# One decoder layer on TensorE: reading the moving operand and writing the result of the block products from the last column to the first

## The chip, the cores and the metric

The kernel runs on one core of one Trainium2 chip, as one program. The time is the device time of one execution in microseconds (us). The time before is the median of two runs. The trace and its page come from one profiled execution; its time is given as its span, from the first to the last instruction.

## The reference, cut to what matters

A hybrid decoder layer over 16 meta tokens and 512 tokens of width 2048, in float32: an input projection, stick-breaking attention in 8 heads beside a gated short convolution of 1024 channels, an output projection and a SwiGLU feed-forward part of width 5632.

```python
n = _rmsnorm(h, g_mix[l])
p = n @ w_in[l]
q, k, v, gb, gc, u = jnp.split(p, ...)
...
o_attn = _stick_breaking_attention(q, k, v).reshape(b, L, ATTN_WIDTH)
o_conv = gb * _causal_dwconv(gc * u, conv_w[l])
o = jnp.concatenate([_rmsnorm(o_attn, g_attn_out[l]), _rmsnorm(o_conv, g_conv_out[l])], axis=-1)
h = h + o @ w_out[l]
n2 = _rmsnorm(h, g_ffn[l])
h = h + (jax.nn.silu(n2 @ w_gate[l]) * (n2 @ w_up[l])) @ w_down[l]
```

Nearly all of the arithmetic is in the products with `w_in`, `w_out`, `w_gate`, `w_up` and `w_down`.

## The kernel before, in words

Everything is kept transposed: 128 channels of one tile lie on the 128 partitions, the tokens along the row. A weight tile of 128 x 128 is the stationary operand of TensorE, activations are the moving operand, and products add up in PSUM over the tiles of the contracted dimension.

Each float32 operand is split into a high part, rounded to the float32r type, and a low part, what the rounding left (`split_quad` for weights, lines 196 to 211: ScalarE casts at line 203, VectorE subtracts at line 206; `split` for activations, lines 352 to 353). A product of two such operands is three matmuls: high by high, high by low, low by high.

The big products also save work in the manner of Strassen's and Winograd's method. Weights and activations are cut into two by two blocks, and seven products of sums of blocks take the place of eight. `pair_product` (line 900) issues the seven in a fixed order into three PSUM banks named `x`, `y` and `z`: `x` gets blocks 0, 2, 4 and 6, `z` gets 1 and 3, `y` gets 5. Between them ScalarE and VectorE read out what has been added up so far. Each of the seven is one call of `block_product` (line 871), the function that the change edits. It takes the next prepared weight block (`next_w`, a running list of pieces, each split some places ahead of its use into the tiles `sw_split`), and for each tile `k` of the contracted dimension issues the three matmuls at lines 887, 890 and 891: `hi` by `ah`, `hi` by `al`, `lo` by `ah`. [...] `act(0, k)` and `act(1, k)` give the high and low part of the moving operand's tile `k`, each with 256 or 258 columns.

The stages that go through `block_product`:

- the convolution pairs (`conv_pair`, `gate_pair`, about 385 to 588 us of the trace): moving operands from the tiles `n` (rows of 528 columns that begin 40 places into their tile) and `mixed`, 258 columns for `conv_pair` and 256 for `gate_pair`;
- gate and up of the feed-forward part (`ffn_pair` from the loop over 44 blocks, about 764 to 1603 us): moving operands `f`, seven sets of eight tiles of 256 columns, which `slots` puts 4 places into their tile;
- down (about 1603 to 2022 us): moving operands `first` and `ring`, four or six tiles of 256 columns, read back from DRAM.

With the quarter of the weights that `two_down` prepares, two output halves lie in one bank of 512 columns and `block_product` loops over both (`m` is 2). The head projections (`product_steps`, lines 340 and 342) and the output projection (`wide_product`, lines 865 to 867) have loops of their own with the same three matmuls, mostly 512 columns wide; they are not edited. In `product_steps` the tile `pq` is made from columns 16 to 528 of the rows `n`. In `gate_pair` the bank `y` is made from columns 16 to 272 of those of them that hold the second half of the channels.

Of the kernel before, what the change touches and what calls it, by code (L numbers as in the profile page):

```python
# [33 lines left out]
def hybrid_layer(ctx: ExitStack, tc: tile.TileContext, xT, w_in, w_out, w_gu, w_down, vecs, out):  # L34
# [269 lines left out]
    def next_w():  # L304
        ahead = max(min(n_first, used[0] + 6), used[0] + 1 + S_AHEAD)
        if used[0] < n_first:
            ahead = min(ahead, n_first + 1)
        while len(split_w) < min(len(pieces), ahead):
            if n_first < len(split_w) <= n_first + S_AHEAD:
                with tc.issue_after(read_q0[3].ins):  # L310
                    prepare()
            else:
                prepare()
        used[0] += 1
        return split_w[used[0] - 1]
# [555 lines left out]
    def block_product(ps, act, start):  # L871

        hi, lo = next_w()
        i = pieces[used[0] - 1][1]
        m = max(1, ps.shape[-1] // T2)
        cols = ps.shape[-1] // m  # L880
        n = pairs[i][0] // m
        for j in range(m):
            p, skip = ps[:, j * cols : (j + 1) * cols], m > 1 or not start
            for k in range(n):
                kk = slice((j * n + k) * P, (j * n + k + 1) * P)
                ah, al = act(0, k), act(1, k)
                opening = pe.matmul(p, hi[:, kk], ah, start=start and j == k == 0, stop=False, skip_group_check=skip)  # L887
                if j == k == 0:
                    tc.keep_in_program_order(opening)
                pe.matmul(p, hi[:, kk], al, start=False, stop=False, skip_group_check=skip)  # L890
                pe.matmul(p, lo[:, kk], ah, start=False, stop=k == n - 1, skip_group_check=skip)  # L891
# [8 lines left out]
    def pair_product(acts, cols, out2, side, fifth=None, hook=None):  # L900
# [16 lines left out]
        if first:  # L917
            block_product(y, acts[5], True)
            go_between()
        block_product(x, acts[0], True)  # L920
        read_out(p1, x)
        go_between()
        if hook:
            hook(1)
        block_product(z, acts[1], True)
        go_between()
        read_out(p5, z)
# [134 lines left out]
    for i, j in enumerate(OUT_TILES):  # L1062
# [36 lines left out]
        ps = ps_out[i]  # L1099
        half, k = divmod(j, 8)  # L1100
# [313 lines left out]
```

## Time and profile before

| what | value |
|---|---|
| median of 2 runs | 2027.59 us (2027.51 to 2027.67) |
| span of the profiled execution | 2025.8 us |
| TensorE: time with a matmul in flight, instructions | 2019.7 us, 16158 |
| weight loads (PEld) | 1961.8 us, 16158 |
| VectorE | 1723.3 us |
| ScalarE | 1077.9 us |
| GpSimd | 337.3 us |
| read from HBM, written to it | 275.78 MB, 77.92 MB |

How to read it. The profile has a row for each instruction: line, engine, operation, the tile written and the tiles read, the shape. Matmuls are pipelined, so the row of one overlaps the next ones' rows: one of 256 columns is in flight for 275 ns, yet the next starts long before that. What a matmul costs the stream is the distance between starts, which is read from the timeline (start times in us) or from a window's length over its count of instructions. Weight loads have rows of their own under the name PEld and overlap the matmuls. In the timeline, rows of one form that follow each other can be merged, with their count after the x.

### The profile page before, as it was taken

Reading aid. Unit: us, or ns where it says so; the run is one execution under the profiler, and the core shown is the slowest. Engines: PE = TensorE matmul, PEld = TensorE weight load, DVE = VectorE, ACT = ScalarE, POOL = GpSimd, SP = SyncE. Lnnn points to the kernel's source line nnn. Section 1 sums busy time; section 2 is a strip of 40 time slices with the busy share of each in tenths; the row PEclk is TensorE's granted clock in tenths of the full one; section 3 lists DMA queues with packets and bytes.
Section 4 is the critical chain, followed back from the end, with each engine's and each line's share of the span. In section 5 each row is a group of like instructions: output and inputs, shape, how many; then the busy total and the mean of one; then the engine's idle time right before and its main releaser. Section 6 shows DMA issues by size and latency. Waiting matters only on the chain.

```text
span 2025.8 us, 39704 instructions
## 1 busy us (share of the span) xinstructions
PE 2019.7 (100%) x16158; PEld 1961.8 (97%) x16158; DVE 1723.3 (85%) x2199; ACT 1077.9 (53%) x1559; POOL 337.3 (17%) x507
## 2 busy tenths in 40 slices
PE   9999999999999999999999999999999999999999
PEld 8999999999998889999999999999999999999999
DVE  7877777698877778999988988988988978888888
ACT  7876676444454445555555555555555544444443
POOL 0111111200014440111110110110110243131211
PEclk9999999999999999999999999999999999999999
DMA  6333343833255555556554554554554999797864
GB/s 222 116 135 115 125 136 136 282 105 110 99 198 179 165 161 194 171 153 186 173 160 148 167 164 149 164 166 151 162 166 151 290 339 352 170 318 193 222 149 91
DMA packets 156664, 356.31 MB, mean 176 GB/s; under 512 B 13696, under 2 KB 68224, under 8 KB 155712
## 3 DMA queue, kind: packets, MB, share of 16 engines
q1 hardware_dynamic: 72640, 216.73, 32.2%
q0 software_dynamic: 83696, 136.99, 25.0%
q8 instruction: 127, 2.08, 0.4%
q14 instruction: 57, 0.47, 0.1%
q10 hardware_dynamic: 144, 0.04, 0.0%
HBM read 275.78 MB, written 77.92 MB: 175 GB/s over the span
## 4 chain that ended last, share of the span: by engine, by line
PE 99%; DMA 0%; DVE 0%; SPq 0%; ACT 0%; issue 0%
PE x L887 14%; PE x L891 14%; PE x L890 14%; PE z L887 7%; PE z L890 7%; PE z L891 7%; PE y L891 3%; PE y L887 3%; PE y L890 3%; PE pk L342 3%; PE pv L342 3%; PE pq L342 3%; PE pv L340 2%; PE pk L340 2%; PE pq L340 1%; PE pb L342 1%
## 5 line engine op out<-in xcount | busy, mean ns | idle before, releaser
L203 ACT CAST sw_split<-sw_in 128x1024 fp32r<-128x1024 f32 (+3 forms) x671 | 662.4, 989 | 708.7 <-PE x L890 174.2
L206 DVE TENSOR_TENSOR sw_split<-sw_in,sw_split 128x1024 fp32r<-128x1024 f32 (+3 forms) x671 | 775.5, 1156 | 140.4 <-ACT sw_split L203 133.0
L887 PE MATMUL x<-f,sw_split 128*128 128x256 f32 x1408 | 387.5, 275 | 0.1
L891 PE MATMUL x<-f,sw_split 128*128 128x256 f32 x1408 | 387.2, 275 | 0.0
L890 PE MATMUL x<-f,sw_split 128*128 128x256 f32 x1408 | 387.2, 275 | 0.0
L887 PEld LDWEIGHTS x<-f,sw_split 128*128 128x128 f32 x1408 | 264.3, 188 | 0.7 <-DVE u L937 0.5
L890 PEld LDWEIGHTS x<-f,sw_split 128*128 128x128 f32 x1408 | 264.3, 188 | 0.0
L891 PEld LDWEIGHTS x<-f,sw_split 128*128 128x128 f32 x1408 | 264.3, 188 | 0.0
L1206 POOL DMA_DIRECT2D fd<-s x147 | 103.7, 921 | 708.0 <-DVE s L353 632.1
L887 PE MATMUL z<-f,sw_split 128*128 128x256 f32 x704 | 193.6, 275 | 0.0
L890 PE MATMUL z<-f,sw_split 128*128 128x256 f32 x704 | 193.6, 275 | 0.0
L891 PE MATMUL z<-f,sw_split 128*128 128x256 f32 x704 | 193.6, 275 | 0.0
L216 DVE TENSOR_TENSOR sw_in<-sw_in 128x1024 f32<-128x1024 f32 (+1 forms) x164 | 187.7, 1145 | 5.4 <-DMA sw_in<-w_in 0.8
L887 PE MATMUL x<-ring,sw_split 128*128 128x256 f32 x608 | 167.2, 275 | 0.0
L890 PE MATMUL x<-ring,sw_split 128*128 128x256 f32 x608 | 167.2, 275 | 0.0
L891 PE MATMUL x<-ring,sw_split 128*128 128x256 f32 x608 | 167.2, 275 | 0.0
L890 PEld LDWEIGHTS z<-f,sw_split 128*128 128x128 f32 x704 | 132.2, 188 | 0.0
L891 PEld LDWEIGHTS z<-f,sw_split 128*128 128x128 f32 x704 | 132.2, 188 | 0.0
L887 PEld LDWEIGHTS z<-f,sw_split 128*128 128x128 f32 x704 | 132.2, 188 | 0.0
L887 PEld LDWEIGHTS x<-ring,sw_split 128*128 128x128 f32 x608 | 114.1, 188 | 0.0
L891 PEld LDWEIGHTS x<-ring,sw_split 128*128 128x128 f32 x608 | 114.1, 188 | 0.0
L890 PEld LDWEIGHTS x<-ring,sw_split 128*128 128x128 f32 x608 | 114.1, 188 | 0.0
(701 smaller groups left out, 5276.9 us busy)
## 6 DMA issues: line engine op xcount, KB each, us to landing
sw_in<-w_gu SPq DMA_DIRECT2D x176, 512.0 KB, 3.8
sw_in<-w_in SPq DMA_DIRECT2D x90, 512.0 KB, 3.3
fd<-s POOLq DMA_DIRECT2D x147, 256.0 KB, 5.1
sw_in<-w_down SPq DMA_DIRECT2D x96, 384.0 KB, 4.2
ring<-fd POOLq DMA_DIRECT2D x42, 768.0 KB, 17.6
sw_in<-w_out SPq DMA_DIRECT2D x32, 512.0 KB, 3.3
out_T<-d POOLq DMA_DIRECT2D x54, 256.0 KB, 4.6
mix_dram<-st_x POOLq DMA_DIRECT2D x16, 516.0 KB, 4.1
```

Of the source, the lines that this page charges most:

```text
L203: cast[0] = sc.copy(hi, src)
L206: latest[0] = ve.tensor_tensor(lo, src, hi.bitcast(F32), ALU.subtract)
L216: return ve.tensor_tensor(sums[name], a, b, ALU.add)
L340: pe.matmul(ps, wh, ah[:, a:b], start=k + i == 0, stop=False)
L342: pe.matmul(ps, w, x[:, a:b], start=False, stop=k + i == last and x is (al if used[0] <= n_first else ah))
L887: opening = pe.matmul(p, hi[:, kk], ah, start=start and j == k == 0, stop=False, skip_group_check=skip)
L890: pe.matmul(p, hi[:, kk], al, start=False, stop=False, skip_group_check=skip)
L891: pe.matmul(p, lo[:, kk], ah, start=False, stop=k == n - 1, skip_group_check=skip)
L1206: gp.dma_start(fd[c][s][:, :, k], t[:, :, i])
```

## The change

In `block_product` the view of the PSUM bank that is written, and the views of both parts of the moving operand, get a step of -1 along the columns. Column 255 of the operand is then read first and its sum is written first, to place 255 of the output; column 0 comes last. Each column's sum goes to the address where it went before. The weights' views, the number of instructions, and all that surrounds the function are the same.

```diff
         n = pairs[i][0] // m
         for j in range(m):
-            p, skip = ps[:, j * cols : (j + 1) * cols], m > 1 or not start
+            p, skip = ps[:, j * cols : (j + 1) * cols][:, ::-1], m > 1 or not start
             for k in range(n):
                 kk = slice((j * n + k) * P, (j * n + k + 1) * P)
-                ah, al = act(0, k), act(1, k)
+                ah, al = (act(i, k)[:, ::-1] for i in range(2))
                 opening = pe.matmul(p, hi[:, kk], ah, start=start and j == k == 0, stop=False, skip_group_check=skip)
```

## The prediction

> **What bounds the kernel now.** I read the page first, parts 1, 2 and 4, to see which engine sets the end.
>
> ```profile
> span 2025.8 us, 39704 instructions
> ...
> PE 2019.7 (100%) x16158; PEld 1961.8 (97%) x16158; DVE 1723.3 (85%) x2199; ACT 1077.9 (53%) x1559; POOL 337.3 (17%) x507
> ...
> PEclk9999999999999999999999999999999999999999
> ...
> PE 99%; DMA 0%; DVE 0%; SPq 0%; ACT 0%; issue 0%
> ```
>
> TensorE is busy in the whole span, its clock is granted at nine tenths or more in every slice (1.00 in the stretches below), and the chain that ended last lies on it for 99%. So the time is a number of matmuls times the distance from one start to the next. That distance, not the mean of one matmul, is the price: neighbours overlap. To get it I asked the view by windows for three stretches in which block products run, first for all instructions, then for those of line 890 alone, one of the three matmul lines of the edited function.
>
> ```profile
> core 0: us, PE busy (x) PEld busy (x) DVE busy (x) ACT busy (x) POOL busy (x), PEclk, DMA share, GB/s
> 385.20:588.00 202.80, 202.65 (x1686) 202.09 (x1685) 175.44 (x201) 98.19 (x129) 5.67 (x10) 1.00 0.41 139
> 764.00:1603.00 839.00, 838.90 (x7397) 838.28 (x7396) 757.57 (x856) 442.68 (x581) 115.11 (x163) 1.00 0.55 168
> 1603.00:2021.90 418.90, 418.90 (x3699) 418.90 (x3697) 364.64 (x467) 197.12 (x285) 89.59 (x106) 1.00 0.85 237
> ```
>
> ```profile
> 385.20:588.00 202.80, 158.28 (x560) 105.91 (x560) 1.00 0.41 139
> 764.00:1603.00 839.00, 677.52 (x2464) 462.56 (x2464) 1.00 0.55 168
> 1603.00:2021.90 418.90, 338.82 (x1233) 231.27 (x1232) 1.00 0.85 237
> ```
>
> Span over count: the convolution pairs (first stretch) take 202.80 us / 1686 = 120.3 ns per matmul, gate and up (second) 839.00 / 7397 = 113.4 ns, down (third) 418.90 / 3699 = 113.2 ns. By the counts of line 890, and three matmul lines, the function issues 3 x 560 = 1,680 matmuls in the first and 3 x (2,464 + 1,232) = 11,088 in the other two: 12,768 of the 16,158, 1,460 of the 2,026 us. A nanosecond on each of them is 12.8 us.
>
> Why do matmuls of one size, 256 columns, come 113 ns apart in one stage and 120 in another? The timeline shows it. First activations of the gate stage (`f`), then tiles `n` in the convolution pairs, twice, then the same `n` tiles with 512 columns in the head loop.
>
> ```profile
> 1002.07 0.28 PE L890 MATMUL z<-f,sw_split 128*128 128x256 f32 x1
> ...
> 1004.45 0.28 PE L890 MATMUL z<-f,sw_split 128*128 128x256 f32 x1
> ```
>
> ```profile
> 460.80 0.29 PE L887 MATMUL x<-n,sw_split 128*128 128x256 f32 x1
> 460.92 0.29 PE L890 MATMUL x<-n,sw_split 128*128 128x256 f32 x1
> 461.05 0.29 PE L891 MATMUL x<-n,sw_split 128*128 128x256 f32 x1
> 461.18 0.28 PE L887 MATMUL y<-n,sw_split 128*128 128x256 f32 x1
> ...
> 461.53 0.28 PE L887 MATMUL y<-n,sw_split 128*128 128x256 f32 x1
> ...
> 463.69 0.28 PE L887 MATMUL y<-n,sw_split 128*128 128x256 f32 x1
> ```
>
> ```profile
> 55.08 0.39 PE L340 MATMUL pq<-n,sw_split 128*128 128x512 f32 x1
> 55.31 0.61 PE L342 MATMUL pq<-n,sw_split 128*128 128x512 f32 x2
> ...
> 57.80 0.39 PE L340 MATMUL pq<-n,sw_split 128*128 128x512 f32 x1
> ```
>
> The 21 steps between the two `z<-f` rows take 2.38 us, 113.3 ns each. The 18 between the two later `y<-n` rows take 2.16 us, 120.0 ns each. The three steps from 460.80 to 461.18 take 0.38 us, 126.7 ns each. The twelve 512-column steps from 55.08 to 57.80 take 2.72 us, 226.7 ns each. The rows of `y` and of `pq` start at the same column of the same kind of tile and differ in length alone, so 256 more columns cost 226.7 - 120.0 = 106.7 ns, 0.417 ns a column. What is left is a fixed part of each matmul with its weight load: 120.0 - 106.7 = 13.3 ns for these reads, 20.0 ns for the ones at 460.80, and 6.7 ns for `f`. The streaming rate is the same; the fixed part goes by which operand is read. My reading, argued and not shown: each matmul hides the next one's weight load (PEld is busy 97%), both read SBUF, and where their reads meet the stream loses some cycles; how often they meet depends on where and in which order the moving operand is read.
>
> **The change, part by part.** Only access patterns change. No instruction, DMA, wait or buffer is added or moved, and no queue is passed by anything. Each output column gets the same sums at the same address, so the readers of PSUM do what they did.
>
> Moving operand, last column first. The columns streamed stay the same in number. If the read keeps its rate, the 106.7 ns stay; what changes is the meeting with the weight load, which keeps its own order. For that fixed part the trace gives the ends. Below: this row, where TensorE takes four 128-column products with their own weight loads.
>
> ```profile
> 53.79 0.60 PE L608 MATMUL va<-ident,v 128*128 128x128 f32 x4
> 54.23 0.27 PE L609 MATMUL vb<-ident,v 128*16 128x128 f32 x1
> ```
>
> They take 54.23 - 53.79 = 0.44 us, 110 ns each, so a weight load does not itself hold products to 113. Above: the 126.7 ns of `x<-n`. Between them lie the 120.0 ns of `y<-n` and the convolution pairs' mean of 120.3 over 1,686. The 113.3 of `f` is the lowest steady value of any 256-column row here, and it is one that was obtained in rising order. I take 120.0, the row of the same shape that is nearest to the mean of all operands not at that low value: 11,088 x (120.0 - 113.4) = +73 us. The convolution pairs are already at such a mean, so I cost them at nothing, with +/-10 us (1,680 x about 6 ns) as the bounds. The cover of these products is unharmed: everything beside them gets more time, and DVE, busiest beside them, had 839.00 - 757.57 = 81 us free in the gate stage.
>
> Result in PSUM, last column first. No row of before writes in falling order, so the cost is bounded only from afar. Below, a write is no slower, zero. Above, it halves the rate: another 106.7 ns for each 256 columns. I take zero, since the 13.3 ns above come out alike for 256 and 512 columns, so the write is not what limits them now, and a falling run touches the same neighbours; the upper end is a rival below.
>
> [...]
>
> Sum: 2025.8 + 73 = 2,099 us of span; the median of the runs, 2027.59, lies 1.8 us above the profiled span, so **2,101 us**. The reads cost more and nothing becomes late, since TensorE is the only engine on the path.
>
> **The rivals.**
>
> No effect: the fixed part depends on where the operand lies, not on its order, so 113.3 stays 113.3. For it: 256 columns cover the same bytes either way, and the `f`, ring and down rows all show that one value although they lie in many places. Against it: `x<-n` at 460.80 and `y<-n` at 461.53, same shape and kind of tile, differ by 6.7 ns, so something finer than shape counts. Time: 2,028 us, 2,018 to 2,038 with the convolution pairs' +/-10.
>
> Halved rate: the read or the write of a falling run goes at one column in two of the present steps. For it: nothing in this trace has been run in falling order, and 0.417 ns a column leaves no slack to hide a slower access. Against it: 256 columns of one row are still neighbours. Price: 12,768 x 106.7 ns = 1,362 us, so 3,390 us. It decides as soon as a column costs visibly more than 0.417 ns; an added 0.1 ns would already make 12,768 x 25.6 ns = 327 us.
>
> Faster: weight load and stream now run through SBUF in an order in which they meet less, so the fixed part falls. For it: 113.3 is not the floor that the 110 ns of `va` show. Against it: in all the `f` and ring rows the low value is the same, which looks like a minimum. Price: at 110 ns the FFN stages give back 11,088 x 3.4 = 38 us and the convolution pairs 1,680 x 10.3 = 17 us: 1,973 us. It decides from 2%, 41 us, on: with the pairs' 17 us the FFN rows must lose 24 us, 2.2 ns each, and without them 3.7 ns, which is 109.7. DVE would then come nearer to being the bound: 757.57 of what would be 814 us, 93%.
>
> [...]
>
> **How the numbers follow.** A few per cent is what has to be told apart, so I count within 2% as no change. More meetings, the forecast: 0.36, its own range 2,040 (the fixed part up by 1.1 ns) to 2,178 (all at 126.7 ns, +151 us). Of this 0.04 lies within 2%. No effect: 0.34, all within 2%. Halved rate: 0.20, all slower. Faster: 0.10, of which 0.01 stays within 2%. So slower 0.32 + 0.20 = 0.52, same 0.04 + 0.34 + 0.01 = 0.39, faster 0.09. The range leaves out the halved rate alone, 0.20: from 1,965, a little under the faster rival, to 2,180.
>
> **What would show it.** Right: the count of instructions stays at 16,158 matmuls, the `z<-f` rows of 256 columns come about 120 ns apart, 764 to 1603 us becomes some 49 us longer and the down stage 24 us, and the 512-column `pq` rows, not edited, stay at 226.7 ns. Wrong: the `f` rows still at 113.3 (no effect); rows over 200 ns apart with a mean well over 275 ns (halved rate); rows near 110 (faster). If the 256- and 258-column rows rise by an amount in proportion to columns, my split into a rate and a fixed part fails; if the matmuls keep 113 ns but idle time appears ahead of them, the whole reading by TensorE alone is wrong.

## The result, and the profile after

The changed kernel takes 2101.46 us (median of 2 runs, 2101.32 to 2101.60) against 2027.59 us: a ratio of 1.0364, interval 1.0334 to 1.0395. It is slower by 73.9 us; the forecast was 2,101 us.

The page after, parts 1 and 4: the same count of instructions on every engine that computes, the same engine on the chain. The span of the profiled execution is 2099.9 us.

```profile
PE 2094.7 (100%) x16158; PEld 2036.5 (97%) x16158; DVE 1732.2 (82%) x2199; ACT 1076.8 (51%) x1559; POOL 338.2 (16%) x507
...
PE 99%; DVE 1%; issue 0%; ACT 0%; DVEq 0%
```

The three stretches by windows, all instructions, with the columns of the windows of before; the granted clock is 1.00 in each, as it was. The last two have the same work as in the windows shown of before; their ends moved to 1652.2 and 2096.1 us.

```profile
385.20:588.00 202.80, 202.65 (x1684) 202.17 (x1683) 174.97 (x200) 97.62 (x128) 5.68 (x10) 1.00 0.41 138
764.00:1652.20 888.20, 888.15 (x7399) 887.71 (x7399) 766.11 (x856) 441.55 (x581) 115.30 (x163) 1.00 0.52 159
1652.20:2096.10 443.90, 443.90 (x3700) 443.75 (x3698) 365.00 (x467) 197.27 (x285) 89.83 (x106) 1.00 0.81 223
```

Span over count: 202.80 / 1684 = 120.4 ns in the convolution pairs (120.3 before), 888.20 / 7399 = 120.0 ns in gate and up (113.4), 443.90 / 3700 = 120.0 ns in down (113.2). Gate and up are 49.2 us longer, down is 25.0 us longer; with nothing from the pairs that makes 74.2, and the span grew by 2099.9 - 2025.8 = 74.1 us. No other group of rows moved the end by as much as 1 us. The timeline, first in the gate stage, then in `gate_pair`, then the 512-column products that were not edited:

```profile
1001.96 0.28 PE L887 MATMUL y<-f,sw_split 128*128 128x256 f32 x1
...
1004.12 0.28 PE L887 MATMUL y<-f,sw_split 128*128 128x256 f32 x1
...
461.03 0.28 PE L887 MATMUL x<-n,sw_split 128*128 128x256 f32 x1
...
461.39 0.28 PE L887 MATMUL y<-n,sw_split 128*128 128x256 f32 x1
...
55.11 0.39 PE L340 MATMUL pq<-n,sw_split 128*128 128x512 f32 x1
...
57.83 0.39 PE L340 MATMUL pq<-n,sw_split 128*128 128x512 f32 x1
```

The 18 steps in `y<-f` take 2.16 us, 120.0 ns each, where 113.3 stood. The last three reads of the block `x<-n` went from 126.7 (at 460.80 before) to 0.36 us / 3 = 120.0 ns. `pq` keeps its 2.72 us for twelve, 226.7 ns. So falling order did not add a constant to what was there: it took the fast rows and some of the slowest ones to the same 120.0 ns.

### The profile page after: what moved, and what is told of

It is laid out like the page before. It is cut to its first block, busy times and chain, and to the rows that moved or that the text cites. A ratio compares the mean times of both kernels' runs of the same rounds, so it can differ in the third digit from the quotient of the medians.

```text
span 2099.9 us, 39735 instructions
## 1 busy us (share of the span) xinstructions
PE 2094.7 (100%) x16158; PEld 2036.5 (97%) x16158; DVE 1732.2 (82%) x2199; ACT 1076.8 (51%) x1559; POOL 338.2 (16%) x507
## 4 chain that ended last, share of the span: by engine, by line
PE 99%; DVE 1%; issue 0%; ACT 0%; DVEq 0%
PE x L887 14%; PE x L891 14%; PE x L890 14%; PE z L887 7%; PE z L890 7%; PE z L891 7%; PE y L891 3%; PE y L887 3%; PE y L890 3%; PE pk L342 3%; PE pv L342 3%; PE pq L342 3%; PE pv L340 2%; PE pk L340 1%; PE pq L340 1%; PE pb L342 1%
## 5 line engine op out<-in xcount | busy, mean ns | idle before, releaser
L887 PE MATMUL x<-f,sw_split 128*128 128x256 f32 x1408 | 400.0, 284 | 0.1
L891 PE MATMUL x<-f,sw_split 128*128 128x256 f32 x1408 | 399.9, 284 | 0.0
L890 PE MATMUL x<-f,sw_split 128*128 128x256 f32 x1408 | 399.9, 284 | 0.0
L887 PE MATMUL z<-f,sw_split 128*128 128x256 f32 x704 | 199.9, 284 | 0.0
L890 PE MATMUL z<-f,sw_split 128*128 128x256 f32 x704 | 199.9, 284 | 0.0
L891 PE MATMUL z<-f,sw_split 128*128 128x256 f32 x704 | 199.9, 284 | 0.0
L887 PE MATMUL x<-ring,sw_split 128*128 128x256 f32 x608 | 172.7, 284 | 0.0
L890 PE MATMUL x<-ring,sw_split 128*128 128x256 f32 x608 | 172.7, 284 | 0.0
L891 PE MATMUL x<-ring,sw_split 128*128 128x256 f32 x608 | 172.7, 284 | 0.0
```

## The experiments

Three theories at the start. Mine: the read of the moving operand meets the weight load's reads in SBUF, and order and place of the read set how often. The rivals: the write in falling order costs it; or falling order costs the read by itself, with no part of the weights in it.

**Read alone, write alone.** Each undoes one half of the change.

```diff
# e1_read                                      (of the changed kernel)
-            p, skip = ps[:, j * cols : (j + 1) * cols][:, ::-1], m > 1 or not start
+            p, skip = ps[:, j * cols : (j + 1) * cols], m > 1 or not start
# e2_write
-                ah, al = (act(i, k)[:, ::-1] for i in range(2))
+                ah, al = act(0, k), act(1, k)
```

> Only the moving operand is read from the last column to the first; the result is written in rising order (so each block's columns come out mirrored). Theory, the read's order against the weight load's: as the changed kernel, 2101 us, within 5 us, and gate-stage rows 120.0 ns apart. Rival, the falling write in PSUM costs the 6.7 ns: as before, 2028 us and rows 113.3 ns apart.

> Only the result is written from the last column to the first; the moving operand is read in rising order (columns mirrored). Theory, the read's order: as before, 2028 us, within 5 us, rows 113.3 ns apart. Rival, the falling write: 2101 us and 120.0 ns.

Read alone: 2101.48 us, ratio 1.0365 (1.035 to 1.038). Write alone: 2027.60 us against 2027.56, ratio 1.000 (0.999 to 1.0009). The gate stage of the one and of the other, in the timeline:

```profile
1001.97 0.28 PE L887 MATMUL y<-f,sw_split 128*128 128x256 f32 x1
...
1004.13 0.28 PE L887 MATMUL y<-f,sw_split 128*128 128x256 f32 x1
```

```profile
1001.88 0.28 PE L887 MATMUL z<-f,sw_split 128*128 128x256 f32 x1
...
1004.26 0.28 PE L887 MATMUL z<-f,sw_split 128*128 128x256 f32 x1
```

18 steps in 2.16 us, 120.0 ns; 21 steps in 2.38 us, 113.3 ns. The whole cost is in the read, none in the write: a written step of -1 did not slow these matmuls.

**Other places, rising and falling.** The operands of the feed-forward stages start at another offset in their tiles, a different one for each slot, so one run shows many. Offsets are in elements from the tile's start; 4 is that of before. The tiles are laid out in multiples of 64 elements (256 bytes), so an offset means the same place against the weights in each of them.

```diff
+    PLACE = {"f0": 0, "f1": 2, "f2": 6, "f3": 8, "f4": 20, "f5": 36, "f6": 52, "first1": 12, ...}
-        t = t[:, 4 : 4 + c].rearrange("p (s a k t) -> p s a k t", s=m, a=2, k=n)
+        at = PLACE.get(name, 4)
+        t = t[:, at : at + c].rearrange("p (s a k t) -> p s a k t", s=m, a=2, k=n)
```

The pad ahead of `f4` had to shrink too, so that slot lies as if at offset 28. The same edit was made to the changed kernel, and both were run again with eighteen further offsets, each version once.

> Rising order as before, but each set of activations of the feed-forward stages starts at another place in its tile (0 to 64 elements instead of 4), so each of the seven block products shows its own distance between matmuls. Theory, the read meets the weight load by place and order: the low 113.3 ns is kept by some places alone, others give 118 to 127 ns; the whole lies between 2040 and 2120 us. Rival, order alone counts: every place shows 113.3 ns, 2028 us.

> The same places, read and written in falling order. Theory, place and order: the distances spread, and at least one place comes near 113.3 ns; 2060 to 2130 us. Rival, order alone: every place shows 120.0 ns, 2101 us.

> Falling order at eighteen further places of the feed-forward operands, odd elements among them. The first scan found 117.7 to 120.1 ns at every place and none at 113.3. Theory, falling order has a cost of its own, 6.7 ns a matmul wherever the operand lies: again all between 117 and 121 ns, 2085 to 2105 us. Rival, falling order only needs another good place: one at least near 113.3 ns.

> Rising order at the same eighteen places. Theory, rising order has no cost of its own and pays by place alone: 117 to 122 ns at most of them, below 115 ns near the two good places of the first scan (16 and 64 bytes below a multiple of 256); 2060 to 2095 us. Rival, only the two places known are good by chance of the row grid: no place below 116 ns.

One block product of the gate stage, rising, and then falling: the first row of the 24 matmuls of `y` (slot 5, offset 36) and the first row of the block behind it, so the difference over 24 is the distance.

```profile
999.88 0.28 PE L887 MATMUL y<-f,sw_split 128*128 128x256 f32 x1
...
1002.69 0.28 PE L887 MATMUL x<-f,sw_split 128*128 128x256 f32 x1
```

```profile
1000.86 0.28 PE L887 MATMUL y<-f,sw_split 128*128 128x256 f32 x1
...
1003.74 0.28 PE L887 MATMUL x<-f,sw_split 128*128 128x256 f32 x1
```

Rising, 2.81 us / 24 = 117.1 ns; falling, 2.88 us / 24 = 120.0 ns. Means over all products of a place, from the timelines of the four runs (ns):

| offset | 0 | 1 | 2 | 3 | 4 | 5 | 6 | 7 | 9 | 28 | 36 | 48 | 52 | 56 |
|---|---|---|---|---|---|---|---|---|---|---|---|---|---|---|
| rising | 119.8 | 120.5 | 120.2 | 119.3 | 113.7 | 121.8 | 121.7 | 119.5 | 123.0 | 119.2 | 117.1 | 117.0 | 118.3 | 113.5 |
| falling | 117.7 | 120.3 | 120.0 | 121.0 | 119.9 | 119.9 | 120.1 | 123.0 | 120.2 | 119.9 | 120.0 | 118.1 | 119.8 | 119.7 |

The runs took 2081.39 (rising) and 2097.20 us (falling), and with the further offsets 2094.75 (rising) and 2107.45 us (falling). In rising order 113 ns belongs to two offsets, 4 and 56, and one element to either side of 4 it is lost: there I had expected less than 115 and was wrong. Elsewhere rising order pays 117 to 123 ns, as much as falling does. In falling order no offset came below the 117.7 of offset 0, with most at 120.0; the further offsets went past my 121 ns and 2105 us. So "order alone" is refuted, for the rising read (113.5 to 123.0 by place) and for the falling one (117.7 to 123.3, the most at offset 63), and "falling only needs another place" found no such place at the 34 offsets tried. Apart from the two low places the ranges of both orders are nearly the same.

**Against what is the place counted?** Weights moved by 16 elements, then weights and operands both (`f`, `ring` and `first` at offset 20 instead of 4).

```diff
-    hpool.tile([P, 24], F32, name="pad_h")
+    hpool.tile([P, 8], F32, name="pad_h")
-    sw_split = sw.tile([P, 6 * 8 * P], F32R, name="sw_split")
+    sw_split = sw.tile([P, 6 * 8 * P + 16], F32R, name="sw_split")[:, 16 :]
# e9_both_shift, besides (the pad ahead of f4 shortened by the room it takes)
-        t = t[:, 4 : 4 + c].rearrange("p (s a k t) -> p s a k t", s=m, a=2, k=n)
+        t = t[:, 20 : 20 + c].rearrange("p (s a k t) -> p s a k t", s=m, a=2, k=n)
```

> Rising order; the split weights lie 16 elements (64 bytes) further on, all else where it was. Theory, what counts is the place of the moving read against that of the weights: the feed-forward rows move to what the scan in rising order showed for operands 64 bytes lower, about 118 ns, and the time to some 2083 us (2065 to 2095). Rival, what counts is the operand's own place: rows stay at 113.3 ns, 2028 us.

> Rising order; weights 64 bytes further on and the activations of the feed-forward stages 64 bytes further on too. Theory, relative place: back to 113.3 ns and within 15 us of 2028 us (the other stages' operands did not move along). Rival, own place: about 118 ns, some 2080 us, as the scan showed near that place.

2089.42 and 2034.31 us. Their timelines, the weights alone moved, and both moved:

```profile
1001.78 0.28 PE L887 MATMUL x<-f,sw_split 128*128 128x256 f32 x1
...
1004.62 0.28 PE L887 MATMUL y<-f,sw_split 128*128 128x256 f32 x1
```

```profile
1001.81 0.28 PE L887 MATMUL x<-f,sw_split 128*128 128x256 f32 x1
...
1004.53 0.28 PE L887 MATMUL z<-f,sw_split 128*128 128x256 f32 x1
```

24 steps in 2.84 us are 118.3 ns, what the rising scan has for operands 16 elements lower (offset 52: 118.3). Moving the operands along brings 2.72 us / 24 = 113.3 ns back. So it is the moving read's place against the weights' that counts, and something that goes to the weight tiles takes part: by my reading the weight load, though the casts and subtractions that fill `sw_split` moved with the tiles too and were not separated from it. Some 7 us stay over in the second run, in products of other stages whose operands were not moved along: 2.8 us of it in the output projection, 2.3 in the 512-column reads of `n`, 2.2 in those of 272 columns.

**Half the weight load.** All but the first and the last matmul of a block load 64 weight columns, and so write 64 rows of the result.

```diff
-                pe.matmul(p, hi[:, kk], al, start=False, stop=False, skip_group_check=skip)
+                pe.matmul(p[:64], hi[:, kk][:, :64], al, start=False, stop=False, skip_group_check=True)
...
```

> Rising order as before, but apart from the first and the last matmul of a block every weight load has 64 columns instead of 128, and the result 64 rows (the other 64 output channels are left out of those sums). The moving read is unchanged. Theory, the fixed part is the stream meeting the weight load's reads: half the load, about half the fixed part, 6.7 to some 3 ns, rows near 110 ns, about 1985 us. Rival, the fixed part belongs to the moving read by itself: rows stay at 113.3 ns, 2028 us.

> The same with 64 weight columns in falling order. Theory: 13.3 halves to some 6.7 ns, rows near 113 ns, about 2025 us. Rival, falling order costs the moving read by itself: rows stay at 120.0 ns, 2101 us.

2064.55 and 2101.47 us. The rising rows (lines 888 to 893 here) and the falling ones:

```profile
1001.90 0.28 PE L891 MATMUL z<-f,sw_split 128*64 128x256 f32 x1
...
1002.95 0.28 PE L891 MATMUL z<-f,sw_split 128*64 128x256 f32 x1
```

```profile
1001.82 0.28 PE L888 MATMUL y<-f,sw_split 128*64 128x256 f32 x1
...
1003.98 0.28 PE L888 MATMUL y<-f,sw_split 128*64 128x256 f32 x1
```

Nine steps in 1.05 us, 116.7 ns; 18 in 2.16 us, 120.0 ns. My theory's number failed in both, and the rival's 113.3 in the rising run. Rising got slower with less to load, so the cost is not in proportion to the weight reads; the shorter load (134 ns in the rows of PEld, not 188) lies otherwise in time beside the stream, and my reading, not tested further, is that the stream lost the good step so. Falling stayed at 120.0, as the rival had it. The halved write went along in both runs and was not separated.

**Longer falling reads.** `product_steps` and `wide_product` turned round as well.

```diff
-                    pe.matmul(ps, wh, ah[:, a:b], start=k + i == 0, stop=False)
+                    pe.matmul(ps[:, ::-1], wh, ah[:, a:b][:, ::-1], start=k + i == 0, stop=False)
...
```

> All projections, the 512-column products of the head loop and of the output projection too, are read and written in falling order. Theory, the falling order's cost comes once for each matmul: the 512-column rows pq stay near 226.7 ns (13.3 above 213.3), and the time within 15 us of 2101. Rival, falling order costs a share of each column: 512 columns get 26.7 ns instead of 13.3, pq rows near 240 ns, and some 1,250 products of 512 columns take 17 us more, about 2118 us.

2108.22 us, and between the numbers of both theories in the rows of `pq`:

```profile
55.31 0.40 PE L340 MATMUL pq<-n,sw_split 128*128 128x512 f32 x1
...
58.11 0.40 PE L340 MATMUL pq<-n,sw_split 128*128 128x512 f32 x1
```

Twelve in 2.80 us, 233.3 ns: 6.7 more than rising, neither 0 nor 13.3. But 233.3 is no mark of falling order. In the run with weights and feed-forward operands moved, the tiles `n` stayed where they were, against weights 64 bytes further on, and `pq` is read in rising order there:

```profile
55.68 0.39 PE L340 MATMUL pq<-n,sw_split 128*128 128x512 f32 x1
...
58.48 0.39 PE L340 MATMUL pq<-n,sw_split 128*128 128x512 f32 x1
```

Twelve in 2.80 us, 233.3 ns as well. So at 512 columns, as at 256, falling order takes what rising order takes at a place that is not a low one, and these rows cannot tell a cost of falling order itself from the loss of the low place. A line through the lowest rows of both lengths, 113.3 and 226.7, has 0.443 ns a column and no fixed part. But those two rows lie at different places, so this line is not shown to be a streaming rate either.

**Can the other stages have the good place?** The `n` tiles start 36 elements earlier, the attention and convolution outputs are moved to offset 56's place.

```diff
-    n_tiles = [npool.tile([P, 2, L + 48], F32R, name=f"n{k}")[:, :, 40:] for k in range(KT)]
+    n_tiles = [npool.tile([P, 2, L + 48], F32R, name=f"n{k}")[:, :, 4:] for k in range(KT)]
-    ocpool.tile([P, 48], F32, name="pad_oc")
+    ocpool.tile([P, 64], F32, name="pad_oc")
-        t = host(m, f"oa{m}")[:, : 4 * SEQ].rearrange("p (h a b) -> p h a b", h=2, a=2)
+        t = host(m, f"oa{m}")[:, 16 : 16 + 4 * SEQ].rearrange("p (h a b) -> p h a b", h=2, a=2)
-    pad(oapool, 128)
+    pad(oapool, 256)
```

> Rising order everywhere; the operands that before did not lie at one of the two good places of the scan (240 and 192 modulo 256 bytes, with the weights at 128) are moved there: the n tiles start 36 elements earlier, the attention and convolution outputs are shifted. Theory, a fixed part for each matmul that goes by relative place: the 512-column pq rows fall from 226.7 to 220.0 ns, and the output projection's rows by 6 to 10 ns; about 1,250 products by some 7 ns and 290 of gate_pair make 8 to 12 us less, 2016 to 2020 us. Rival, the low value belongs to the feed-forward stage (to 256 columns or to what runs beside it): pq stays at 226.7 ns and the time at 2028 us.

2034.44 us, ratio 1.0032 (1.002 to 1.0044): 0.3% longer, against the gain that I expected, and within the 2% that the prediction counts as no change. In the timeline, `gate_pair` and the head loop:

```profile
464.74 0.28 PE L887 MATMUL y<-n,sw_split 128*128 128x256 f32 x1
...
466.16 0.28 PE L887 MATMUL y<-n,sw_split 128*128 128x256 f32 x1
...
470.24 0.28 PE L887 MATMUL x<-n,sw_split 128*128 128x258 f32 x1
...
55.34 0.39 PE L340 MATMUL pq<-n,sw_split 128*128 128x512 f32 x1
...
58.12 0.39 PE L340 MATMUL pq<-n,sw_split 128*128 128x512 f32 x1
```

Most of the 256-column reads of `n` did get there: after twelve steps with a mean of 118.3 ns (464.74 to 466.16) the next 36 take 4.08 us, 113.3 ns each, and it goes the same way in all three gate pairs. So the low value is found outside the feed-forward stages too, though the stream can take some steps to fall into it. But at that same place 512 columns take 2.78 us / 12 = 231.7 ns, where the old one had 226.7. Summed by rows, the 256-column reads of `n` in `gate_pair` gain 1.5 us; the longer reads of `n` lose, 2.0 us with 258 columns, 1.1 with 272 and 1.6 with 512, and the output projection loses 3.7. A place that is good for one length need not be good for another. No version beat the kernel before.

## Why the prediction was right, point by point

- *TensorE alone sets the end, 12,768 products at their distance.* Right: the 49.2 and 25.0 us of the two stretches named make up the 74.1 us, at the same matmul count.
- *11,088 products go from 113.4 to 120.0 ns, +73 us.* Right in size: 120.0 and 120.0 measured. The value was taken as that of operands not at the low value, and the scans bear that out: away from offsets 4 and 56 rising order takes 117 to 123 ns as well.
- *To the microsecond it was luck.* The row that lent its 120.0 ns, `y<-n`, itself went to 118.5 under the change, and falling reads at other offsets take 117.7 to 123.3. With the operands at offset 0 the same sum would have been some 25 us smaller (11,088 x 2.3 ns). That falling order leaves every operand at offset 4 at 120.0 was not foreseen, and the forecast itself had only 0.36 against 0.34 for no effect.
- *The `f`, ring and down rows show one value "although they lie in many places".* Wrong: `slots` puts all of them at offset 4, one and the same place against the weights. What the argument for "no effect" took as independence of place was a single place, and one element off it the rising read takes 119 to 122 ns.
- *The convolution pairs at nothing, +/-10 us.* Right: 120.3 and 120.4 ns. Inside them the forecast hid movements that nearly cancel. In `gate_pair` the slow block `x<-n` went from 126.5 down to 120.0 ns, the blocks of `mixed` from 118.0 up to 120.1, and the other blocks of `n` from 119.9 down to 118.4.
- *The write at zero.* Right, shown by the write alone (ratio 1.000). The reason given was not one: that 13.3 ns "come out alike" for 256 and 512 columns follows from drawing one line through those two rows. No run shows a halved rate, the rival's term: 256 columns took 113.3 ns with the falling write and 120.0 with the falling read.
- *A streaming rate of 0.417 ns a column and a fixed part of 13.3, 20.0 or 6.7 ns.* Not borne out. I compared `y` and `pq`, which begin at the same column, as though place acted alike on 256 and 512 columns; it does not. With the `n` tiles moved the same two rows take 113.3 and 231.7 ns, which would be 0.462 ns a column. What part is rate and what part is lost stays open. The sum did not suffer, as it used the difference of 120.0 and 113.4 alone. The faster rival, priced at 110 ns, found no row: no place and no order gave 256 columns a steady distance under 113.3.
- *The upper end of the forecast's own range, +151 us.* Slightly off: 11,088 x 13.3 ns is 147 us. Nothing hangs on it.
- *The fixed part is the stream meeting the weight load.* Half borne out; no row shows the two meet. For rising reads the place against the weights decides (118.3 with the weights moved, 113.3 with both). But the cost is not in proportion to what is loaded, and the falling read's 120.0 ns did not react to half a load. Whether falling order has a cost of its own, or merely misses the low state at every place tried, stays open. A weight load read in the other direction was not tried.

## What to carry to other kernels

Where TensorE is busy throughout, price a matmul by the distance of starts in steady rows of its own shape, and look whether rows of the same shape have other distances elsewhere in the trace: a row at the lowest of them can be in a state that an edit to the access pattern loses, as the rows of `f` were. The falling read, of the same bytes by the same instructions, cost 6% of a stage (113.3 to 120.0 ns a matmul, 839.00 to 888.20 us for gate and up). Change the read and the write of a matmul one at a time, and tune the place of an operand for the very length that is streamed: the place that gave 256 columns 113.3 ns gave 512 columns 231.7, against 226.7 where they lay before.

## What the runs showed of the hardware that was not expected

A place one element off costs as much as any other (offset 3: 119.3, 4: 113.7, 5: 121.8 ns, rising). Loading half as many weights, for half as many rows of the result, made rising matmuls slower (113.3 to 116.7 ns). The stream can take some steps to settle: twelve with a mean of 118.3 ns before a run at 113.3. A 512-column read that took 226.7 ns takes 233.3 with nothing changed for it but the place of the weights. And a falling write in PSUM was free (2027.60 against 2027.56 us).
